# Decode step taken apart (new states made in the later convolutions and the inner out pairs) and 16 K tiles by Strassen in the heads

## The chip, the cores and the metric

One core of a Trainium2 chip runs the whole program. The metric is the device time of one execution in microseconds. The kernel before takes 2169.63 us, the median of three runs (2169.62 to 2169.96).

## The reference, cut to what matters

Two layers of a decoder trunk are run for a prompt of 512 tokens and for 8 decode samples of one token each; both share all weights, so the kernel carries 520 columns. Each layer has a wide input projection (8192 columns of K = 2048), a short convolution, a retention with 4 heads of 256, an output projection and a gate.

```python
def retention_chunk(S, q, k, v, log_gamma):
    ...
    scores = jnp.einsum('blhd,bmhd->bhlm', q, k) * decay[None]
    intra = jnp.einsum('bhlm,bmhe->blhe', scores, v)
    q_dec = jnp.exp(log_gamma[None, :] * (idx[:, None] + 1.0))
    inter = jnp.einsum('blhd,bhde->blhe', q, S) * q_dec[None, :, :, None]
    k_dec = jnp.exp(log_gamma[None, :] * (L - 1.0 - idx[:, None]))
    S_new = (jnp.exp(log_gamma * L)[None, :, None, None] * S
             + jnp.einsum('blhd,blhe->bhde', k * k_dec[None, :, :, None], v))
    return S_new, intra + inter

def trunk_layer(x, p_i, pos, conv_buf, ret_S, norm_g, w_in, conv_w, gn_g, w_out, w_pg, w_ple):
    h = rmsnorm(x, norm_g)
    z = h @ w_in
    ...
    y_conv = b_c * conv_y * jax.nn.silu(g_c)
    ...
    o, new_S = retention(q, k, v, ret_S.astype(jnp.float32), retention_log_gamma())
    ...
    x = x + jnp.concatenate([y_conv, y_ret], axis=-1) @ w_out
    x = x + jax.nn.sigmoid(x @ w_pg) * (p_i @ w_ple)
```

For a decode sample L is 1. Its new state is S' = gamma S + k v, and its output is o = q S'. There are 64 such states (2 layers x 4 heads x 8 samples), each 256 x 256 floats, 256 KB.

## The kernel before, in words

**Matmuls.** The operands stay in SBUF, transposed: 16 K tiles of 128 rows by 520 columns (512 tokens and 8 samples, in a LEFT and a RIGHT half of 260). A product in full precision is three matmuls: high part of the weights by high and by low part of the operand, and low part by high part (`mm3`, L247 to L249). A weight is loaded by SP into the ring `raw` (32 tiles), and split by ACT (`hi`, L229) and DVE (`lo`, L230) into the ring `split` (60 tiles). One call of `pair` makes two blocks of 128 output rows from two rows of weights. Its number `s` in the lists HEADS, CONVS, OUT_ROWS and GATES says how many of the 16 K tiles go through one level of Strassen's scheme: 7 products of s/2 tiles, and 4 sums of weights, which DVE adds in `raw` (L319) before they are split. The other 16 - s tiles go through four plain products. With s = 0 (`plain`) there is no scheme.

**Stages of a layer.** First the heads: 16 pairs (four per head: q, k, v, gate), with DVE and ACT work for rope, and the retention of the prompt in nine small steps per head, which `aside` takes from the list `later` in the middle and at the end of each pair. Then the convolutions: 8 steps j, each with two pairs. Then the out pairs (m = 0, 2, ..., 14), of which the first and the last have s = 0, then the gate pairs. Between stages the operands of the next one are built from tiles that POOL loads (`Operands.fill`, `build`: yc and ys for the out pairs), as slots come free. 75 slots of 128 x 520 hold operands, tiles and states.

**The decode step.** After a head's v is there, `todo` gets its 8 states. `sample` is called once or twice in a pair through the heads and the convolutions: it works on the state that was loaded at the call before, and loads the next one. A state needs two slots: the state (L770), and k and q of the sample, broadcast to all partitions (L771). ACT multiplies the state by gamma (L776), DVE adds k v in two halves (L780), POOL stores the new state (L781), and DVE multiplies it by q and sums (L784) into `osum`. `sample_norm`, in the last convolution, normalizes `osum` for the out pairs.

**What sets the order.** Each engine runs its instructions in one order, fixed when the program is built: a scheduler places them by their place in the code, by priorities (`WPRIO` puts weight splits ahead) and by its own estimate of when inputs are ready. `keep` pins an instruction behind what was traced before it on its engine. `middle` and `later` are lists of calls that a pair takes up at fixed points in it. SP's queue loads weights alone, but for the start and the end; all other loads and stores are issued by POOL, in one queue.

Of the kernel before, what the change touches and what calls it, by code (L numbers as in the profile page):

```python
# [7 lines left out]
F32 = mybir.dt.float32  # L8
# [5 lines left out]
P = 128  # L14
# [38 lines left out]
HEADS = [[0, 0, 0, 8] + [14] * 12, [0] + [14] * 15]  # L53
CONVS = [[14] * 2 + [16] * 13 + [14]] * 2
# [10 lines left out]
SPLIT = 60  # L65

# [125 lines left out]
def trunk_kernel(  # L192
# [368 lines left out]
    vec = const.tile([P, 160], F32, name="vec")  # L561
# [18 lines left out]
    def gam(h):  # L580
        return vec[:, 128 + h : 129 + h]

# [7 lines left out]
    osum = const.tile([P, 2, H, NS], F32, name="osum")  # L590
    gs = const.tile([P, 2 * H, NS], F32, name="gs")
# [83 lines left out]
    for a, b in ((0, 1), (1, 4), (4, 8), (8, 12), (12, 16)):  # L675
        raws = []
        if b == 1:
            raw = raw_ring.get(4)
            DMA.dma_start(raw.rearrange("p (m n) -> p m n", n=P), wi[0, 0:4, :, :P].rearrange("m p n -> p m n"))
            S.dma_start(vec, vecs)  # L680
# [35 lines left out]
    for l in range(DEPTH):  # L716
# [51 lines left out]
        def sample_load(h, b):  # L768
            st, kb = get(), get()
            SIDE.dma_start(st[:, :512], sret[l, h, b])  # L770
            SIDE.dma_start(kb[:, :512], kq[l, h, b].rearrange("c d -> (c d)").partition_broadcast(P))  # L771
            return h, b, st, kb

        def sample_step(h, b, st, kb):

            keep(S.activation(st[:, :512], st[:, :512], AF.Identity, scale=gam(h)))  # L776
            k = kb[:, 256:512]
            for e in range(2):
                c = slice(256 * e, 256 * e + 256)
                keep(V.scalar_tensor_tensor(st[:, c], k, vs[:, h, e, b : b + 1], st[:, c], MUL, ADD))  # L780
            SIDE.dma_start(o_rets[l, h, b], st[:, :512])  # L781
            for e in range(2):
                c = slice(256 * e, 256 * e + 256)
                V.tensor_tensor_reduce(k, st[:, c], kb[:, :256], 1.0, 0.0, MUL, ADD, osum[:, e, h, b : b + 1])  # L784
            put(st, kb)

        loaded = []
# [7 lines left out]

        todo = []
# [20 lines left out]
        def retain(h):  # L817
# [21 lines left out]
            aside_copy(h, 2, kf)  # L839
            qkt = small.tile([P, 4, 32], F32, tag="qkt", name="qkt")  # L840
# [6 lines left out]
            for e, z in enumerate(head(mt + 4)):  # L847
                t = z.slot if z.ps is None else copied(z.ps).slot
                V.scalar_tensor_tensor(vs[:, h, e, :], t[:, SEQ:T], 1.0 / 16, rb[:, SEQ:T], MUL, MUL)
# [227 lines left out]
        for j in range(CJ):  # L1077
            mt = 32 + 4 * j
            O.ready = min(j // 2, 3)
            middle.append(sample)  # L1080
            zc, zx = pair(X, wi[l], mt, mt // 2 - skipped, O)
            u = get()
# [18 lines left out]
            if j == CJ - 1:  # L1101
# [3 lines left out]
                sample_norm(nc, small, pr, osum, onesd, half_neg, gs, lambda k: gn_g(l, k))  # L1105
            zg, zb = pair(X, wi[l], mt + 2, mt // 2 + 1 - skipped, O)
            gt = silu(zg)
# [371 lines left out]
```

## Time and profile before

| | |
|---|---|
| median of three runs | 2169.63 us |
| span of the profiled execution, first to last instruction | 2167.3 us |
| PE busy | 2147.8 us |
| DVE busy | 1896.1 us |
| ACT busy | 1264.5 us |
| POOL busy | 430.6 us |
| read from HBM, written to it | 318.96 MB, 65.15 MB |

The profiled execution is given by its span; the 2.3 us between it and the median lie around it. By the lines that mark the stages, the heads of the first layer run to about 460 us, its convolutions to 710, its out pairs to 870 and its gates to 1110; the second layer's to about 1540, 1785, 1945 and 2130 us. Busy time of a matmul counts its whole way through the array, so that overlapping ones fill an engine's row; the counts (x) of a stretch tell how many were started. The granted clock is 1.00 of full speed in the stretches that are read below.

### The profile page before, as it was taken

What the parts mean: (1) busy time and instruction counts of PE and PEld (TensorE: products, weight loads), DVE (VectorE), ACT (ScalarE), POOL (GpSimd) and SP (SyncE); (2) the same over time, 40 slices, a digit from 0 to 9 for tenths busy, and PEclk for the clock granted to TensorE, in tenths of its full rate; (3) what the DMA queues carried; (4) which work ended last, traced back from release to release, by engine and by line L of the source; (5) the groups of instructions that cost most, each with busy time, mean ns of one, the idle gap of its engine ahead of it and who ended that gap; (6) DMA issues with size and microseconds to landing.
All of it is one profiled execution on the core that took longest, in us unless ns stands there. A gap on an engine that the chain in (4) does not pass through costs nothing. (4 is left out here: it accounts for less than half of the span.)

```text
span 2167.3 us, 48178 instructions
## 1 busy us (share of the span) xinstructions
PE 2147.8 (99%) x17861; PEld 2142.1 (99%) x17861; DVE 1896.1 (87%) x3849; ACT 1264.5 (58%) x2647; POOL 430.6 (20%) x746
## 2 busy tenths in 40 slices
PE   9999999999999999999999999999999999999998
PEld 9999999999999999999999999999999999999998
DVE  8889988998999987987997988989999998879884
ACT  8656655565555655655765655565645555456565
POOL 2313222211001211200212222231111022011011
PEclk9999999999999999999999999999999999999999
DMA  8555565545543745645645566664464355566455
GB/s 288 171 175 197 181 217 184 178 157 175 158 129 118 238 156 187 215 154 160 215 144 175 172 213 191 189 209 170 151 182 149 120 158 202 176 207 200 128 164 198
DMA packets 182861, 387.31 MB, mean 179 GB/s; under 512 B 25888, under 2 KB 56352, under 8 KB 182624
## 3 DMA queue, kind: packets, MB, share of 16 engines
q1 hardware_dynamic: 128704, 212.98, 31.6%
q0 software_dynamic: 53056, 169.84, 23.8%
q8 instruction: 140, 2.29, 0.4%
q10 hardware_dynamic: 864, 1.39, 0.2%
q14 instruction: 97, 0.79, 0.1%
HBM read 318.96 MB, written 65.15 MB: 177 GB/s over the span
## 5 line engine op out<-in xcount | busy, mean ns | idle before, releaser
L247 PE MATMUL ps_g<-slot,split 128*128 128x260 f32 x5465 | 1531.6, 284 | 7.2 <-ACT slot L307 2.9
L248 PE MATMUL ps_g<-slot,split 128*128 128x260 f32 x5465 | 1534.3, 282 | 0.3 <-DVE slot L555 0.3
L249 PE MATMUL ps_g<-slot,split 128*128 128x260 f32 x5461 | 1519.9, 283 | 0.5 <-DVE split L230 0.5
L229 ACT ACTIVATE split<-raw 128x512 fp32r<-128x512 f32 (+2 forms) x1347 | 777.3, 596 | 583.1 <-DVE raw L319 213.2
L247 PEld LDWEIGHTS ps_g<-slot,split 128*128 128x128 f32 x5465 | 1024.0, 188 | 10.1 <-ACT slot L307 3.7
L248 PEld LDWEIGHTS ps_g<-slot,split 128*128 128x128 f32 x5465 | 1028.5, 188 | 0.5 <-DVE slot L555 0.5
L249 PEld LDWEIGHTS ps_g<-slot,split 128*128 128x128 f32 x5461 | 1019.8, 188 | 1.0 <-DVE split L230 1.0
L230 DVE TENSOR_TENSOR split<-raw,split 128x512 fp32r<-128x512 f32 (+2 forms) x1346 | 849.2, 652 | 172.5 <-PE ps_g L248 85.4
L319 DVE TENSOR_TENSOR raw<-raw 128x512 f32<-128x512 f32 (+1 forms) x660 | 428.9, 660 | 32.5 <-DMA raw<-wi 23.7
L307 ACT ACTIVATE slot<-ps_g 128x260 f32<-128x260 f32 x336 | 127.4, 381 | 140.6 <-PE ps_g L249 122.7
L551 ACT ACTIVATE slot<-slot 128x520 fp32r<-128x520 f32 (+1 forms) x212 | 109.2, 562 | 46.6 <-DVE slot L414 11.1
L552 DVE TENSOR_TENSOR slot<-slot,slot 128x520 fp32r<-128x520 f32 (+1 forms) x212 | 124.4, 620 | 4.1 <-ACT slot L551 3.9
L781 POOL DMA_DIRECT2D o_rets<-slot x64 | 35.3, 552 | 351.6 <-DVE slot L780 131.7
L307 DVE TENSOR_TENSOR slot<-ps_g,slot 128x260 f32<-128x260 f32 x168 | 70.9, 424 | 6.0 <-PE ps_g L249 3.7
L869 POOL DMA_DIRECT2D slot<-hs x64 | 46.2, 724 | 118.7 <-DVE split L230 42.7
L814 POOL DMA_DIRECT2D hs<-slot x64 | 35.6, 556 | 139.3 <-DVE slot L755 61.3
L780 DVE SCALAR_TENSOR_TENSOR slot<-slot,vs,slot 128x256 f32<-128x256 f32 x128 | 56.1, 481 | 4.5 <-ACT slot L776 4.3
L746 DVE TENSOR_TENSOR slot<-slot,slot 128x520 f32<-128x520 f32 x80 | 55.8, 698 | 4.7 <-DMA o_rets<-slot 3.7
L770 POOL DMA_DIRECT2D slot<-sret x64 | 35.5, 554 | 114.6 <-ACT split L229 37.3
L1058 POOL DMA_DIRECT2D slot<-x1s x76 | 40.8, 538 | 87.6 <-PE ps_g L249 27.2
L1209 POOL DMA_DIRECT2D x2s<-slot x30 | 16.4, 545 | 201.6 <-DVE slot L1204 200.6
L771 POOL DMA_DIRECT2D slot<-kq x64 | 34.9, 547 | 106.0 <-DVE slot L876 22.2
(217 smaller groups left out, 1733.8 us busy)
## 6 DMA issues: line engine op xcount, KB each, us to landing
raw<-wi SPq DMA_DIRECT2D x377, 256.0 KB, 3.9
raw<-wo SPq DMA_DIRECT2D x128, 256.0 KB, 5.4
raw<-wg SPq DMA_DIRECT2D x122, 256.0 KB, 4.1
raw<-wi SPq DMA_DIRECT2D x136, 192.0 KB, 4.0
slot<-x1s POOLq DMA_DIRECT2D x76, 260.0 KB, 5.1
slot<-sret POOLq DMA_DIRECT2D x64, 256.0 KB, 4.0
hs<-slot POOLq DMA_DIRECT2D x64, 256.0 KB, 4.0
slot<-hs POOLq DMA_DIRECT2D x64, 256.0 KB, 5.2
```

Source lines behind the costliest of these rows:

```text
L229: S.activation(hi, raw, AF.Copy)
L230: V.tensor_tensor(lo, raw, F(hi), SUB)
L247: PE.matmul(out, wh, xh, start=start, stop=False, skip_group_check=more)
L248: PE.matmul(out, wh, xl, start=False, stop=False, skip_group_check=more)
L249: PE.matmul(out, wl, xh, start=False, stop=stop, skip_group_check=more)
L307: fn(*args)
L319: V.tensor_tensor(out[:, n], x[:, n], y[:, n], op)
L551: keep(S.activation(hi, src[:, n], AF.Copy))
L552: V.tensor_tensor(lo, src[:, n], F(hi), SUB)
L746: V.tensor_tensor(out[:, n], v, table[:, n], MUL)
L780: keep(V.scalar_tensor_tensor(st[:, c], k, vs[:, h, e, b : b + 1], st[:, c], MUL, ADD))
L869: SIDE.dma_start(t[:, :512].rearrange("p (m n) -> p m n", m=2), src)
```

## The change

The decode step is taken apart. With gamma folded into v (`vs` holds v / 16 / gamma), the new state is gamma (S + k v'), and the output is gamma q S + (gamma q k) v'.

- **Output.** `sample` loads the state alone, and the q of two samples at once (one slot for two states). DVE multiplies by q with the factor gamma and sums, twice per state; nothing is written to the state but the product. The part of k v' is added for all samples at once in `sample_norm`: two products of ones by `qk` on PE, and four small DVE operations.
- **New state.** `update` makes it later: in the convolutions from j = 3 twice in a pair, in the out pairs m = 2 to 12 three times. A call loads the broadcast k of one state (L798, `key_load`), multiplies the k that the call before had loaded by v' on ACT, half by half (L804), and issues a DMA that adds the old state from HBM to it in SBUF (L805, `accum_op=ADD`). Two calls after that ACT multiplies by gamma (L809) and POOL stores the state (L810).
- **Strassen.** 14 becomes 16 in 12 head pairs of the first layer and 15 of the second, and in the first two convolution pairs of both.

```diff
+GAMMA = [1.0 - 2.0 ** (-5 - h) for h in range(H)]
-HEADS = [[0, 0, 0, 8] + [14] * 12, [0] + [14] * 15]
-CONVS = [[14] * 2 + [16] * 13 + [14]] * 2
+HEADS = [[0, 0, 0, 8] + [16] * 12, [0] + [16] * 15]
+CONVS = [[16] * 15 + [14]] * 2
...
+UPDATES = 3
...
         def sample_load(h, b):
-            st, kb = get(), get()
+            st = get()
             SIDE.dma_start(st[:, :512], sret[l, h, b])
-            SIDE.dma_start(kb[:, :512], kq[l, h, b].rearrange("c d -> (c d)").partition_broadcast(P))
-            return h, b, st, kb
-
-        def sample_step(h, b, st, kb):
-
-            keep(S.activation(st[:, :512], st[:, :512], AF.Identity, scale=gam(h)))
-            k = kb[:, 256:512]
+            if b % 2 == 0:
+                queries.append(get())
+                src = kq[l, h, b : b + 2, :2].rearrange("b c d -> b (c d)").partition_broadcast(P)
+                SIDE.dma_start(queries[-1][:, :512].rearrange("p (b c) -> p b c", b=2), src)
+            return h, b, st, queries[-1]
+
+        def sample_step(h, b, st, q):
+
             for e in range(2):
                 c = slice(256 * e, 256 * e + 256)
-                keep(V.scalar_tensor_tensor(st[:, c], k, vs[:, h, e, b : b + 1], st[:, c], MUL, ADD))
-            SIDE.dma_start(o_rets[l, h, b], st[:, :512])
-            for e in range(2):
-                c = slice(256 * e, 256 * e + 256)
-                V.tensor_tensor_reduce(k, st[:, c], kb[:, :256], 1.0, 0.0, MUL, ADD, osum[:, e, h, b : b + 1])
-            put(st, kb)
-
-        loaded = []
+                n = slice(256 * (b % 2), 256 * (b % 2) + 256)
+                keep(V.tensor_tensor_reduce(st[:, c], st[:, c], q[:, n], GAMMA[h], 0.0, MUL, ADD, osum[:, e, h, b : b + 1]))
+            put(st)
+            if b % 2:
+                put(q)
...
+        def key_load(h, b):
+            st = get()
+            SIDE.dma_start(st[:, 256:512], kq[l, h, b, 2:].rearrange("c d -> (c d)").partition_broadcast(P))
+            return h, b, st
+
+        def state_add(h, b, st):
+            for e in range(2):
+                c = slice(256 * e, 256 * e + 256)
+                keep(S.activation(st[:, c], st[:, 256:512], AF.Copy, scale=vs[:, h, e, b : b + 1]))
+            SIDE.dma_start(st[:, :512], sret[l, h, b], accum_op=ADD)
+            return h, b, st
+
+        def state_out(h, b, st):
+            keep(S.activation(st[:, :512], st[:, :512], AF.Copy, scale=GAMMA[h]))
+            SIDE.dma_start(o_rets[l, h, b], st[:, :512])
+            put(st)
+
+        keyed, added = [], []
+
+        def update():
+
+            if len(added) > 1 or added and not (keyed or states):
+                state_out(*added.pop(0))
+            if keyed:
+                added.append(state_add(*keyed.pop(0)))
+            if states:
+                keyed.append(key_load(*states.pop(0)))
...
+            V.scalar_tensor_tensor(qk[:, :, h], qks[:, :2, :NS], GAMMA[h], qks[:, 2:, :NS], MUL, MUL)
...
+            if j >= UPDATES:
+                middle.append(update)
             zc, zx = pair(X, wi[l], mt, mt // 2 - skipped, O)
+            if j >= UPDATES:
+                update()
...
+            busy = 0 < m < KT - 2
+            if busy:
+                middle.append(update)
+                later.append(update)
             zs = pair(O, wo[l], m, m // 2, Gt)
+            if busy:
+                update()
...
+    for d in range(2):
+        PE.matmul(ps[:, :n], ones, qk[:, d].rearrange("p h b -> p (h b)"), start=d == 0, stop=d == 1)
+    own = small.tile([P, 2, H, NS], F32, tag="sq", name="own", bufs=1)
+    for e in range(2):
+        V.tensor_tensor(own[:, e], vs[:, :, e], ps[:, :n].rearrange("p (h b) -> p h b", b=NS), MUL)
+        V.tensor_tensor(osum[:, e], osum[:, e], own[:, e], ADD)
```

**How it moves instructions.** On DVE, in a head pair of the first layer, before: weight splits of 3 and 4 tiles (128x384, 128x512) and of the two plain tiles (128x256), and between them a decode step with its add (L780) and its two products (L784, each followed by a read of its sum).

```order
L230 TENSOR_TENSOR split_73<-raw_72,split_73 128x512
L230 TENSOR_TENSOR split_73<-raw_72,split_73 128x384
L984 SCALAR_TENSOR_TENSOR shift_2030<-mv_2027,rstp_2029 128x2
L230 TENSOR_TENSOR split_73<-raw_72,split_73 128x512
L780 SCALAR_TENSOR_TENSOR slot65_174_1910<-slot30_175_1911,vs_81,slot65_174_1910 128x256 x2
L230 TENSOR_TENSOR split_73<-raw_72,split_73 128x256 x2
L784 ISA slot30_175_1911,osum_82<-slot65_174_1910,slot30_175_1911 128x256
```

On DVE at such a place of the change (its lines are shifted: L232 is L230, L321 is L319, L782 is L784):

```order
L232 TENSOR_TENSOR split_73<-raw_72,split_73 128x512
L948 SCALAR_TENSOR_TENSOR slot65_196_2319<-ps_kt_2313,vec_74,slot60_195_2318 128x256
L782 ISA slot10_181_2015,osum_82<-slot10_181_2015,slot56_182_2017 128x256
L782 ISA osum_82 128x1
L782 ISA slot10_181_2015,osum_82<-slot10_181_2015,slot56_182_2017 128x256
L782 ISA osum_82 128x1
L232 TENSOR_TENSOR split_73<-raw_72,split_73 128x512 x5
L321 TENSOR_TENSOR raw_72<-raw_72 128x512
```

The adds and the pieces of 2 and 3 tiles are gone; all pieces have 4 tiles.

On POOL, where the convolutions of the first layer go over into the out pairs, the row of the change holds loads of yc and ys (operands of the out pairs), loads of xT (their residuals), and of the update the store o_rets, the accumulating load from sret and the key load from kq:

```order
L810 DMA o_rets<-slot65_447_8721 128x512
L1093 DMA slot44_516_9362<-ys_93 128x512
L1171 DMA slot46_542_9695<-xT 128x520
L1088 DMA slot53_526_9542<-yc_89 128x520
L805 DMA slot68_452_8965<-sret 128x512
L1171 DMA slot52_525_9427<-xT 128x520
L1093 DMA slot0_532_9557<-ys_93 128x512
L1093 DMA slot70_531_9554<-ys_93 128x512
L1171 DMA slot45_541_9694<-xT 128x520
L810 DMA o_rets<-slot14_451_8900 128x512
L805 DMA slot38_493_9254<-sret 128x512
L798 DMA slot11_522_9417<-kq_92 128x256
```

Before, POOL's row holds there the loads of yc, ys and xT alone:

```order
L1058 DMA slot21_477_9343<-yc_88 128x520
L1058 DMA slot29_478_9345<-yc_88 128x520
L1118 DMA o_conv<-ncv_79 128x144
L1063 DMA slot59_490_9374<-ys_92 128x512
L1063 DMA slot66_489_9371<-ys_92 128x512
L1063 DMA slot20_508_9501<-ys_92 128x512
```

On ACT, in an out pair of the change (L231 are the weight splits, L309 copies out of PSUM, L553 operand splits), one state, slot52_554, from its two copies with v' to its last copy:

```order
L804 ACTIVATE slot52_554_9818<-slot52_554_9818,vs_81 128x256
L231 ACTIVATE split_73<-raw_72 128x512 x2
L309 ACTIVATE slot47_543_9702<-ps_g_9700 128x260
L804 ACTIVATE slot52_554_9818<-slot52_554_9818,vs_81 128x256
L553 ACTIVATE slot67_558_9977<-slot0_556_9971 128x520
L553 ACTIVATE slot44_560_9981<-slot58_557_9972 128x520
L231 ACTIVATE split_73<-raw_72 128x512 x3
L309 ACTIVATE ps_g_10009<-ps_g_10007 128x260
L231 ACTIVATE split_73<-raw_72 128x512
L809 ACTIVATE slot52_554_9818<-slot52_554_9818 128x512
```

Four weight splits stand between the second L804, on which the accumulating DMA waits, and L809, which waits for that DMA. Before, none of the L804 and L809 rows are there, and nothing in their place.

More of the change, by code (lines that the diff above doesn't have):

```diff
@@ L558, in split @@
         return op
-    vec = const.tile([P, 160], F32, name="vec")
+    vec = const.tile([P, P], F32, name="vec")
     def norm_g(l, k):
@@ L578, in kd @@
         return vec[:, c : c + 1]
-    def gam(h):
-        return vec[:, 128 + h : 129 + h]
     ident = const.tile([P, P], F32, name="ident")
@@ L590, in trunk_kernel @@
     osum = const.tile([P, 2, H, NS], F32, name="osum")
+    qk = const.tile([P, 2, H, NS], F32, name="qk")
     gs = const.tile([P, 2 * H, NS], F32, name="gs")
@@ L679, in trunk_kernel @@
             DMA.dma_start(raw.rearrange("p (m n) -> p m n", n=P), wi[0, 0:4, :, :P].rearrange("m p n -> p m n"))
-            S.dma_start(vec, vecs)
+            S.dma_start(vec, vecs[:, :P])
             x = get()
@@ L768, in sample_load @@
         def sample_load(h, b):
[L769 removed]
+            st = get()
             SIDE.dma_start(st[:, :512], sret[l, h, b])
[L771 to L777 removed]
+            if b % 2 == 0:
[4 more added lines that the diff above has]
+        def sample_step(h, b, st, q):
             for e in range(2):
                 c = slice(256 * e, 256 * e + 256)
[L780 to L787 removed]
+                n = slice(256 * (b % 2), 256 * (b % 2) + 256)
[3 more added lines that the diff above has]
+                put(q)
+        loaded, queries = [], []
         def sample():
@@ L794, in sample @@
                 loaded.append(sample_load(*todo.pop(0)))
+        def key_load(h, b):
[20 more added lines that the diff above has]
+                keyed.append(key_load(*states.pop(0)))
+        states = [(h, b) for h in range(H) for b in range(NS)]
         todo = []
@@ L1104, in trunk_kernel @@
                 O.ready = 7
-                sample_norm(nc, small, pr, osum, onesd, half_neg, gs, lambda k: gn_g(l, k))
+                sample_norm(nc, small, pr, osum, qk, vs, ones, onesd, half_neg, gs, lambda k: gn_g(l, k))
+            if j >= UPDATES:
+                middle.append(update)
             zg, zb = pair(X, wi[l], mt + 2, mt // 2 + 1 - skipped, O)
+            if j >= UPDATES:
+                update()
             gt = silu(zg)
@@ L1135, in trunk_kernel @@
             middle.append(lambda: O.fill(MORE_OUT, 0))
+            busy = 0 < m < KT - 2
+            if busy:
+                middle.append(update)
+                later.append(update)
             zs = pair(O, wo[l], m, m // 2, Gt)
+            if busy:
+                update()
             for i, (x, z) in enumerate(zip(xs, zs)):
@@ L1359, in trunk_kernel, with sample_norm @@
             block_out(1)
+        assert not (todo or loaded or states or keyed or added)
         if l < DEPTH - 1:
             X.ready = KT // 2
-def sample_norm(nc, small, pr, osum, onesd, half_neg, gs, gn):
+def sample_norm(nc, small, pr, osum, qk, vs, ones, onesd, half_neg, gs, gn):
     V, G, PE = nc.vector, nc.gpsimd, nc.tensor
@@ L1368, in sample_norm @@
     flat = osum.rearrange("p e h b -> p e (h b)")
+    ps = pr.tile([P, 512], F32, tag="r", name="ps_qk")
+    for d in range(2):
[4 more added lines that the diff above has]
+        V.tensor_tensor(osum[:, e], osum[:, e], own[:, e], ADD)
     ps = pr.tile([P, 512], F32, tag="r", name="ps_sm")
```

2 lines of the change are left out of this document (1 added, 1 removed).

## The prediction

> **What bounds the kernel now.** I read the engine shares first, then the busy times by stretch, then the groups by form, and last the DMA answer.
>
> ```profile
> PE 2147.8 (99%) x17861; PEld 2142.1 (99%) x17861; DVE 1896.1 (87%) x3849; ACT 1264.5 (58%) x2647; POOL 430.6 (20%) x746
> ```
>
> PE is busy 99%, but matmuls overlap, so this alone could hide a PE that is fed late. Starts per stretch decide. In the rows below the columns are stretch, length, then PE, weight load, DVE, ACT and POOL busy with their counts, granted clock, DMA share, GB/s.
>
> ```profile
> 640.00:660.00 20.00, 20.00 (x170) 20.00 (x169) 18.64 (x38) 10.98 (x21) 1.08 (x2) 1.00 0.46 133
> 1060.00:1080.00 20.00, 20.00 (x169) 20.00 (x168) 19.80 (x46) 18.98 (x38) 5.87 (x11) 1.00 0.78 258
> 1080.00:1100.00 20.00, 20.00 (x169) 20.00 (x168) 19.85 (x44) 18.51 (x37) 5.88 (x11) 1.00 0.72 230
> ```
>
> PE starts 169 or 170 matmuls in 20 us whether DVE is busy 18.6 or 19.85 of them, ACT 11 or 19, DMA 0.46 or 0.78. So the pace is PE's own: 20 us / 169 = 118.3 ns a matmul, and a matmul less is 118.3 ns less as long as feeding holds. Where it doesn't hold is seen in few places; the worst are the changes from the convolutions to the out pairs, one in each layer (700 and 1780 us).
>
> ```profile
> 700.00:730.00 30.00, 26.68 (x218) 26.07 (x218) 30.00 (x65) 24.88 (x68) 10.58 (x20) 1.00 0.81 272
> 1780.00:1800.00 20.00, 18.15 (x149) 17.72 (x149) 19.66 (x44) 13.67 (x38) 6.77 (x13) 1.00 0.94 333
> ...
> 720.00:726.00 6.00, 5.30 (x45) 5.10 (x43) 6.00 (x13) 6.00 (x18) 2.31 (x5) 1.00 1.03 376
> 726.00:732.00 6.00, 4.58 (x35) 4.37 (x36) 6.00 (x14) 4.14 (x12) 1.07 (x2) 1.00 0.98 357
> ```
>
> PE loses 3.3 us in the first and 1.85 us in the second. There the DMA engines are full (1.03, 0.98), DVE has no gap and ACT is full for 6 us at a time.
>
> **16 tiles by Strassen, on PE.** A pair with s = 14 issues 7 products of 7 tiles and 2 tiles in four plain products, 3 matmuls each: 147 + 24 = 171. With s = 16 it is 7 x 8 x 3 = 168. The lists change 27 pairs in the heads and 2 per layer in the convolutions: 31 x 3 = 93 matmuls, and 93 x 118.3 ns = **-11.0 us**, all on PE's path.
>
> **The same on DVE.** It pays for it:
>
> ```profile
> L230 DVE TENSOR_TENSOR split<-raw,split 128x512 fp32r<-128x512 f32 x1031 | 695.0, 690 | 147.8 <-PE ps_g L248 81.2 <-ACT split L229 51.8 <-issue 6.1
> L319 DVE TENSOR_TENSOR raw<-raw 128x512 f32<-128x512 f32 x520 | 354.1, 688 | 17.6 <-DMA raw<-wi 12.1 <-DMA raw<-wo 2.9
> L230 DVE TENSOR_TENSOR split<-raw,split 128x384 fp32r<-128x384 f32 x249 | 137.1, 555 | 16.2 <-ACT split L229 9.9 <-PE ps_g L248 3.4 <-ACT slot L551 1.9
> L319 DVE TENSOR_TENSOR raw<-raw 128x384 f32<-128x384 f32 x140 | 77.4, 554 | 14.9 <-DMA raw<-wi 11.6 <-DMA raw<-wg 2.8
> L780 DVE SCALAR_TENSOR_TENSOR slot<-slot,vs,slot 128x256 f32<-128x256 f32 x128 | 56.1, 481 | 4.5 <-ACT slot L776 4.3
> ...
> L230 DVE TENSOR_TENSOR split<-raw,split 128x256 fp32r<-128x256 f32 x66 | 27.3, 423 | 8.5 <-ACT split L229 7.6 <-PE ps_g L248 0.8
> ```
>
> Splits per pair: 7 x (690 + 555) + 2 x 423 = 9.56 us before, 14 x 690 = 9.66 us after. Sums of weights: 4 x (688 + 554) = 4.97 us before, 8 x 688 = 5.50 us after. That is 0.64 us more in each of 31 pairs, 19.8 us. The decode step gives back its two L780 a state: 128 x 481 ns = 61.6 us by means (56.1 busy, since they overlap). Where they run (DVE busy with L780 alone):
>
> ```profile
> 66.00:410.00 344.00, 17.57 (x40) 1.00 0.59 190
> ...
> 1110.00:1480.00 370.00, 17.56 (x40) 1.00 0.59 184
> ```
>
> So DVE does some 36 us less in all (56.1 - 19.8), and in the heads 27 x 0.64 = 17 us more against 35 less.
>
> ```profile
> 66.00:460.00 394.00, 394.00 (x3289) 393.53 (x3288) 357.23 (x774) 234.63 (x515) 102.58 (x178) 1.00 0.58 185
> 460.00:710.00 250.00, 247.85 (x2069) 247.48 (x2068) 228.30 (x454) 138.68 (x282) 36.67 (x54) 1.00 0.49 148
> 710.00:870.00 160.00, 157.88 (x1314) 157.45 (x1313) 134.96 (x248) 85.92 (x183) 26.82 (x50) 1.00 0.60 195
> ```
>
> DVE has 37 us idle in the first head stage already (394 - 357), and the convolutions ran 13 of their 16 pairs with s = 16 beside 228 of 250 us of DVE. I cost the DVE part at nothing; if that cover were gone it would be 17 us, and the 35 us stand against it. No more slots are taken: the operands are shared with the convolutions, whose rows of 16 had all eight sums built before.
>
> **The state update on ACT and POOL.** Per state ACT loses one L776 early and gains two half copies with a scale and one full copy later. The trace doesn't have these; the nearest rows:
>
> ```profile
> L776 ACT ACTIVATE slot<-slot,vec 128x512 f32<-128x512 f32 x64 | 45.7, 714 | 0.0
> L917 ACT ACTIVATE slot<-ps_kt,vec 128x256 fp32r<-128x256 f32 x32 | 15.0, 468 | 9.2 <-DMA hs<-slot 3.2 <-DVE slot L918 2.5 <-PE ps_kt L913 2.2
> L874 ACT ACTIVATE slot<-slot 128x512 fp32r<-128x512 f32 x48 | 28.7, 624 | 10.1 <-DMA yc<-slot 4.6 <-DVE slot L904 2.4 <-DVE osum L784 2.1
> L770 POOL DMA_DIRECT2D slot<-sret x64 | 35.5, 554 | 114.6 <-ACT split L229 37.3 <-PE ps_s L249 13.8 <-ACT slot L307 9.7
> ```
>
> 2 x 468 + 624 = 1.56 us an update (1.65 with L776's for the last copy). An out pair has up to three calls: 4.7 us beside 85.9 / 160 x 20 = 10.7 us of ACT in 20. ACT holds that. POOL issues 96 more DMAs (64 accumulating, 64 of keys, 32 of queries for 64 of L771): 96 x 554 ns = 53 us of an engine that is idle 80%. Hidden. What is new is who waits: the accumulating DMA waits on POOL for ACT's two copies, the store of o_rets for its last one, and behind them in POOL's queue stand key loads, the residual loads of the out pairs and their x1s stores, for which the next pair's slots wait.
>
> **The DMA engines.**
>
> ```profile
> q0 software_dynamic: 53056, 169.84, 23.8%
> ...
> slot<-sret POOLq DMA_DIRECT2D x64, 256.0 KB, 4.0
> ```
>
> Queue 0 moves 169.84 MB in 23.8% of 16 engines' span: 0.238 x 2167.3 / 169.84 = 3.04 us a MB, or 0.80 us for 256 KB. An accumulating DMA isn't in this trace. It reads HBM, and SBUF too: 0.80 us if the second read is free, 1.6 us if it costs a load and a store. I take 0.80, its nearest row, and keep both.
> The Trainium skill (Collectives: The Full Stack, "The bandwidth ceiling: the fold count and why AG ≠ RS ≠ AR") says that an adding transfer is slow not by its add but by its two source reads; by that the upper value holds, and no row here shows it. By that rule the sum below would be about 2 x 2.4 us higher, 2169 us.
>
> An update moves 256 + 256 + 128 KB: 2.0 us. In the convolutions (DMA 0.49) and in the out pairs (0.60) that is 3 x 2.0 = 6 us in 20, up to 0.9 of the engines, about what 1060 us has without loss. I cost it at nothing there.
>
> At the **change of stage** it isn't free. By the order, between the store of o_conv and that of the last yc, POOL issues three o_rets stores, three accumulating DMAs and four key loads: 6 x 0.80 + 4 x 0.40 = 6.4 us (8.8 by the upper value). The 30 us from 700 have 0.19 x 30 = 5.7 us of DMA idle and 5.1 of ACT, and three updates need 4.7 of ACT. So it just fits on paper, in a stretch where PE waits anyway and yc and ys loads stand behind o_rets in one POOL queue. Loss: at best less than now (the order has fewer operand splits ahead of the last convolution's copies on ACT), at worst all 8.8 us. I take 2.5 us in each layer, near the overflow (0.7 to 3.1), **+5.0 us**.
>
> **The small sums.** ps_qk adds 8 small matmuls:
>
> ```profile
> L1371 PE MATMUL ps_sm<-osum,onesd x8: 191/275/276, 664.7 to 1734.8; 128*128 128x32 f32 x8
> ```
>
> They overlap, and have an eighth of the columns of a matmul of 118.3 ns; I take 90 ns each, **+0.7 us** (0 to 8 x 0.275 = 2.2). The order has ps_sm 800 matmuls behind ps_qk, so the four small DVE rows between are waited for by nobody.
>
> **Sum**, on the profiled execution: 2167.3 - 11.0 + 0.7 + 5.0 = 2162.0. Its span is 2.3 us below the median of the runs, 2169.6; I carry that along: **2164 us**.
>
> **The rivals.**
> *The change of stage costs nothing:* for it speak 1060 to 1100 us, as loaded and without loss. 2167.3 - 11.0 + 0.7 + 2.3 = 2159.3.
> *It costs twice as much:* loads queue behind o_rets stores that wait for ACT, which waits for an accumulating DMA. 5.5 us a layer: 2170. For it: DMA at 1.03 there already.
> *The added wait becomes the bound (slower).* On ACT the last copy of a state waits for its accumulating DMA, and behind it on ACT stand the weight splits that PE needs. By the order 17 states have seven splits or fewer between the two, often five; 14 splits go to a pair of 19.9 us, so five are 7.1 us.
>
> ```profile
> L770 POOL DMA_DIRECT2D slot<-sret x64: 537/544/585, 50.5 to 1670.9; - x64
> ...
> DMA to landing us min/median/max: 2.8/4.0/7.3
> ```
>
> A plain load lands in 4.0 us, 7.3 at most, and at that nothing waits. But an out pair has 20 - 15.4 = 4.6 us of ACT idle and 1.4 such states: from a landing of 7.1 + 4.6 / 1.4 = 10.4 us on PE falls behind, by 1.4 x 12 pairs = 17 us for each us more. The point from which the kernel is slower than before is 10.7 us; at 12 us it costs 27 us: 2191. Against it: that is 2.6 times a plain load's median.
> *DVE sets the pace, not PE* (the 93 matmuls then count for nothing, and the change works by DVE): the heads would shorten by up to 35 - 17 = 18 us, 2155. The steady 169 starts speak against it.
>
> **How the numbers follow.** Forecast 0.38, no cost at the change 0.22, twice the cost 0.24, the slower rival 0.13, DVE 0.03. A measurement of this kernel can tell about 0.2% (4.3 us) from no change: faster is below 2165.3, slower above 2174.0. Faster gets 0.22, 0.03 and 0.30 of the forecast's 0.38: 0.55. Same gets the other 0.08 and most of the doubled cost: 0.31. Slower gets 0.13 and a rest: 0.14. The range runs from the rival without cost, less 3 us if PE loses less there than the 3.3 and 1.85 us of now, 2156, to the doubled cost with the upper bound of the DMAs (2167.3 - 11.0 + 0.7 + 2 x 8.8 + 2.3 = 2176.9), 2177.
>
> **What would show it.** PE rows fall by 85 (93 - 8), with 118.3 ns still between starts, and pairs in the heads at 19.9 us. DVE busy falls by about 36 us, ACT rises. In the 30 us around 700 and 1780 PE's loss grows from 3.3 and 1.85 by some 2.5 each. The accumulating DMAs land in 4 to 8 us, and ACT waits for few of them. I am wrong if the head stages lose PE time, if landings pass 10 us, or if the out pairs show PE idle where they had none.

## The result and the profile after

The changed kernel takes 2202.76 us (median of five runs, 2196.15 to 2209.13), the kernel before 2169.63 in the same job (five runs, 2166.32 to 2169.96). The ratio is 1.016 with a 95% interval of 1.0141 to 1.0179: slower by 33 us, and 39 us above the forecast. The sign was wrong, and the time lies outside the range. Two executions on record, one of experiment 2 (5762.05 us) and one of experiment 5 (7419.09 us), ran in a slower state of the chip and are left out of the times below.

The page of the changed kernel, first its engine shares, then its two large DMA queues (packets, MB, share of 16 engines; q1 carries SP's transfers, the weights, and q0 POOL's, states, keys and activations):

```profile
PE 2149.2 (98%) x17776; PEld 2136.5 (97%) x17776; DVE 1876.2 (85%) x3675; ACT 1299.8 (59%) x2682; POOL 512.4 (23%) x842
...
q1 hardware_dynamic: 119776, 212.98, 30.1%
q0 software_dynamic: 62784, 186.63, 28.0%
```

PE has the 85 rows less that were expected (17861 - 17776) and DVE 20 us less (36 were forecast), so no engine has grown into a bound by its sum. Queue 0 has grown from 23.8% to 28.0%, and in a longer span.

To find the place I took the starts of three landmark rows of DVE: the second shifted product of the first and of the last convolution of a layer (L1093 before, L1127 after), and the last addition of its residual in the out pairs (L1139, L1183). They cut the profiled execution into stages, in us. These landmarks are rows of DVE, and PE's own stream moves a little against them, so the last two columns count the matmuls that PE starts in a stage, and PE's lost time: the length of the stage less 118.3 ns for each matmul started.

| stage | before | after | difference | matmuls, difference | lost time, difference |
|---|---|---|---|---|---|
| start to the first convolution (heads of layer 0) | 411.7 | 406.9 | -4.8 | -55 | +1.7 |
| convolutions, layer 0 | 303.4 | 306.3 | +2.9 | -12 | +4.2 |
| last convolution to the last out pair, layer 0 | 182.1 | 200.2 | +18.1 | +32 | +14.3 |
| gates of layer 0 and heads of layer 1 | 585.6 | 576.2 | -9.4 | -79 | -0.2 |
| convolutions, layer 1 | 300.2 | 307.1 | +6.9 | +8 | +6.0 |
| last convolution to the last out pair, layer 1 | 184.1 | 204.4 | +20.3 | +10 | +19.2 |
| the rest | 200.2 | 200.0 | -0.2 | +11 | -1.5 |

The heads gained 14 us, but only because PE starts 134 matmuls fewer between their landmarks (15.9 us); the lists of 16 explain 81 of them (27 pairs x 3, 9.6 us). Time is lost where the updates are: 10.2 us in the convolutions and 33.5 in the two stages of out pairs. The same columns as in the prediction, for stretches of the change:

```profile
1060.00:1110.00 50.00, 50.00 (x420) 50.00 (x419) 44.36 (x96) 42.70 (x85) 14.93 (x28) 1.00 0.81 263
...
570.00:700.00 130.00, 126.99 (x1044) 125.58 (x1042) 109.81 (x213) 78.05 (x166) 34.03 (x43) 1.00 0.62 175
...
690.00:760.00 70.00, 63.21 (x493) 61.38 (x491) 55.83 (x123) 43.77 (x107) 27.98 (x39) 0.95 0.71 231
730.00:740.00 10.00, 8.03 (x42) 7.27 (x43) 10.00 (x24) 9.70 (x25) 1.98 (x3) 0.66 1.04 337
...
780.00:850.00 70.00, 64.36 (x521) 62.70 (x520) 53.16 (x92) 44.82 (x95) 25.72 (x42) 1.00 0.82 226
```

And the kernel before in four of these stretches:

```profile
570.00:700.00 130.00, 130.00 (x1088) 130.00 (x1087) 118.98 (x237) 69.53 (x138) 12.39 (x13) 1.00 0.43 130
...
690.00:760.00 70.00, 66.68 (x552) 66.05 (x551) 63.57 (x132) 42.21 (x104) 17.12 (x32) 1.00 0.67 215
730.00:740.00 10.00, 10.00 (x86) 10.00 (x85) 9.30 (x20) 3.97 (x10) 2.77 (x6) 1.00 0.65 193
...
780.00:850.00 70.00, 70.00 (x586) 70.00 (x585) 57.53 (x96) 34.38 (x65) 6.46 (x12) 1.00 0.49 160
```

From 690 to 760 us, around the change from convolutions to out pairs, PE starts 493 matmuls instead of 552. Part of that is the clock: behind PE's waits there its granted clock has a mean of 0.66 from 730 to 740 us (42 matmuls, 86 before), and 0.95 over the 70 us, which is 3.5 us of full clock. In the kernel before it is 1.00.

From 780 to 850 us PE starts 521 matmuls instead of 586. No engine is full there: DVE has 53 of 70 us, ACT 45. The DMA engines went from 0.49 to 0.82. But 0.81 costs nothing at 1060 us, so the share alone doesn't say it. The DMA answer, cut to a stretch of convolutions, shows more (issues, KB each, median us from issue to landing). Before, from 570 to 700 us:

```profile
raw<-wi SPq DMA_DIRECT2D x47, 256.0 KB, 3.5
```

After, in the same stretch:

```profile
raw<-wi SPq DMA_DIRECT2D x44, 256.0 KB, 6.5
slot<-sret POOLq DMA_DIRECT2D x15, 256.0 KB, 6.5
```

The weights land 3 us later. The sum of two weights on DVE, which is the first to touch a landed weight (L319 before, L321 after), shows it as idle time; for wi and wo together 26.6 us before, 55.6 after:

```profile
L319 DVE TENSOR_TENSOR raw<-raw 128x512 f32<-128x512 f32 (+1 forms) x660 | 428.9, 660 | 32.5 <-DMA raw<-wi 23.7 <-DMA raw<-wo 2.9 <-DMA raw<-wg 2.8
L321 DVE TENSOR_TENSOR raw<-raw 128x512 f32<-128x512 f32 (+1 forms) x660 | 441.7, 680 | 59.2 <-DMA raw<-wi 36.6 <-DMA raw<-wo 19.0 <-DMA raw<-wg 0.5
```

One such place, from the chain of waits of the change between 825 and 850 us (start, us, what):

```profile
831.25 0.69 DVE split L232
831.97 9.33 DMA raw<-wo
841.55 0.44 issue
842.00 0.43 DVE slot L309
842.47 0.39 PE ps_g L249
```

A load of weights took 9.33 us, and PE went on only behind it. That is one place; in the out pairs the median landing hardly moves (5.8 us before and 6.1 after, from 780 to 850 us). What waits for the adding transfer itself is small. All instructions of its line (L805), who waited for them, and their landing:

```profile
L805 POOL DMA_DIRECT2D slot<-sret x64: 849/882/1272, 537.8 to 1950.0; - x64
...
  ACT slot L809: 13.0, 7
...
DMA to landing us min/median/max: 4.0/6.7/11.2
```

So after the first look two theories stood: the adding transfers crowd the weights out (A), or the waits of ACT and POOL behind them pass on to PE (B, the prediction's slower rival). The letters in the expectations below are each run's own. And Strassen's part had to be priced by itself.

### The profile page after: what moved, and what is told of

The parts are those of the page before. It is cut to its first block, busy times and chain, and to the rows that moved or that the text cites. A ratio compares the mean times of both kernels' runs of the same rounds, so it can differ in the third digit from the quotient of the medians.

```text
span 2201.0 us, 47748 instructions
## 1 busy us (share of the span) xinstructions
PE 2149.2 (98%) x17776; PEld 2136.5 (97%) x17776; DVE 1876.2 (85%) x3675; ACT 1299.8 (59%) x2682; POOL 512.4 (23%) x842
## 4 chain that ended last, share of the span: by engine, by line
PE 75%; DMA 10%; DVE 5%; issue 5%; ACT 3%; POOL 1%; DVEq 0%; SPq 0%; POOLq 0%; ACTq 0%
PE ps_g L249 23%; PE ps_g L251 23%; PE ps_g L250 23%; DMA raw<-wi 5%; DMA raw<-wo 2%; DVE split L232 2%; DVE raw L321 2%; ACT split L231 1%; DMA slot<-yc 1%; ACT slot L804 1%; DMA slot<-sret 1%; ACT slot L809 1%; PE ps_p L249 1%; PE ps_p L250 1%; PE ps_p L251 1%
## 5 line engine op out<-in xcount | busy, mean ns | idle before, releaser
L231 ACT ACTIVATE split<-raw 128x512 fp32r<-128x512 f32 (+1 forms) x1285 | 779.5, 623 | 555.0 <-DVE raw L321 306.7
L249 PEld LDWEIGHTS ps_g<-slot,split 128*128 128x128 f32 x5434 | 1018.9, 188 | 47.8 <-DVE slot L309 14.6
L232 DVE TENSOR_TENSOR split<-raw,split 128x512 fp32r<-128x512 f32 x1284 | 851.7, 680 | 190.7 <-PE ps_g L250 97.6
L321 DVE TENSOR_TENSOR raw<-raw 128x512 f32<-128x512 f32 (+1 forms) x660 | 441.7, 680 | 59.2 <-DMA raw<-wi 36.6
L309 ACT ACTIVATE slot<-ps_g 128x260 f32<-128x260 f32 x336 | 128.2, 382 | 159.7 <-PE ps_g L251 140.3
L553 ACT ACTIVATE slot<-slot 128x520 fp32r<-128x520 f32 (+1 forms) x212 | 109.4, 562 | 40.4 <-DVE slot L416 10.9
L309 DVE TENSOR_TENSOR slot<-ps_g,slot 128x260 f32<-128x260 f32 x168 | 70.6, 421 | 5.1 <-PE ps_g L251 4.8
L770 POOL DMA_DIRECT2D slot<-sret x64 | 35.7, 559 | 160.3 <-ACT split L231 24.6
L805 POOL DMA_DIRECT2D slot<-sret x64 | 57.3, 895 | 67.6 <-ACT slot L804 36.8
L810 POOL DMA_DIRECT2D o_rets<-slot x64 | 36.8, 575 | 135.6 <-ACT slot L809 125.5
L798 POOL DMA_DIRECT2D slot<-kq x64 | 37.5, 587 | 132.4 <-DMA o_rets<-slot 46.6
L804 ACT ACTIVATE slot<-slot,vs 128x256 f32<-128x256 f32 x128 | 63.7, 498 | 1.1 <-DMA slot<-kq 1.1
L1088 POOL DMA_DIRECT2D slot<-x1s x76 | 41.1, 542 | 87.8 <-PE ps_g L251 33.5
```

What stands on the lines that cost most here:

```text
L231: S.activation(hi, raw, AF.Copy)
L232: V.tensor_tensor(lo, raw, F(hi), SUB)
L249: PE.matmul(out, wh, xh, start=start, stop=False, skip_group_check=more)
L309: fn(*args)
L321: V.tensor_tensor(out[:, n], x[:, n], y[:, n], op)
L553: keep(S.activation(hi, src[:, n], AF.Copy))
```

## The experiments

Each ratio is to the kernel before in the same job; the medians of before were 2168.92 (the first four), 2168.60 (the next three), 2168.46 (the next three) and 2167.44 us (the last).

**1. A plain load in place of the adding one.** The instructions stand in the same order on every engine.

```diff
-            SIDE.dma_start(st[:, :512], sret[l, h, b], accum_op=ADD)
+            SIDE.dma_start(st[:, :512], sret[l, h, b])
```

> The changed kernel with a plain load of the old state in place of the accumulating one; the order of every engine's instructions is the same, row for row. The new states lack the k v part. Theory A (the accumulating DMA itself: it lands later, 6.7 us by median against 3.9 for the plain sret loads of the decode step, and holds back the weight loads beside it, 6.4 against 4.1 us): the 44 us between the forecast and the change go for the most part, 2160 to 2172 us. Theory B (the added traffic of 256 KB and 128 KB loads at that place, whatever their kind): 2190 us or more. Theory C (added rows on ACT and waits in POOL's queue): 2190 us or more.

2178.52 us, ratio 1.0056 (1.0035 to 1.0078), between the theories. The adding alone is worth 24.2 us of the 33, but the rest is more than theory A expected: a plain second load isn't free either.

**2. No second load at all.** The line is left out.

```diff
-            SIDE.dma_start(st[:, :512], sret[l, h, b], accum_op=ADD)
```

> The changed kernel without the second load of the old state (the new states are k v alone); the scheduler places other instructions anew. Theory A: as with the plain load, within 5 us of it, 2158 to 2170 us. Theory B: only this one gets near 2160 us, the plain load doesn't. Theory C: 2185 us or more, since ACT's rows and the stores in POOL's queue remain.

2166.96 us, ratio 0.9994 (0.9984 to 1.0004). The plain load is 11.6 us of the change, the adding load 35.8. Theory C is out; of A and B neither holds as it stands, since both the load and its kind count. From 780 to 850 us this kernel starts 585 matmuls, as before, with the key loads, both kinds of copies on ACT and the o_rets stores in place:

```profile
780.00:850.00 70.00, 70.00 (x585) 69.93 (x584) 58.09 (x98) 45.93 (x95) 18.38 (x34) 1.00 0.67 217
```

But the rest of the change isn't free. This kernel, too, starts 85 matmuls fewer than the kernel before, 10.1 us, and its span is only 0.8 us shorter (2166.5 for 2167.3). So PE loses 9.3 us more than before without any second load, 3.3 and 7.0 us of it in the stages of out pairs (190.1 and 193.7 us). Whether keys, copies, stores or the order make that wasn't taken apart.

**3. Strassen's lists alone, in the kernel before.**

```diff
-HEADS = [[0, 0, 0, 8] + [14] * 12, [0] + [14] * 15]
-CONVS = [[14] * 2 + [16] * 13 + [14]] * 2
+HEADS = [[0, 0, 0, 8] + [16] * 12, [0] + [16] * 15]
+CONVS = [[16] * 15 + [14]] * 2
```

> The kernel before with the Strassen lists of the change alone. If PE sets the pace and DVE's gaps hold the 17 us that the heads' pairs add: 93 matmuls less, 2159 us. If DVE has no room in the heads without the decode step's relief: 2167 us or more.

2186.00 us, ratio 1.0077 (1.0057 to 1.0096): 17.1 us slower, where 11 us were to be gained. The loss lies in the heads: start to the first convolution 422.5 us (before 411.7), gates and heads of layer 1 592.7 (585.6). The first heads of this kernel:

```profile
66.00:400.00 334.00, 324.09 (x2666) 321.98 (x2665) 301.29 (x614) 189.29 (x388) 92.32 (x158) 0.99 0.56 184
```

And of the kernel before:

```profile
66.00:400.00 334.00, 334.00 (x2788) 333.53 (x2787) 301.68 (x659) 199.83 (x441) 93.16 (x162) 1.00 0.59 190
```

DVE is busy for the same 301 us of 334 and PE starts 122 matmuls fewer beside it. Its 33 us idle were no room for more work; what held them open wasn't taken apart. The granted clock is 0.99 here, 3 us of full clock in 334.

**4. The change with the old lists.** The same four lines the other way.

> The change with the Strassen lists of before, so the decode step alone. If the two parts add up, it is the 2203 us of the change plus 11: 2208 to 2218 us. If the longer pairs with 16 have a part in the loss: below 2203 us.

2206.28 us, ratio 1.018 (1.0159 to 1.02). That lies between the two cases that were expected. By the medians the lists of 16 bring the change 3.5 us, but the intervals of the two ratios overlap. Its two head stages take 408.5 and 581.0 us, so 7.8 of the 14 us that the heads gained come with the decode step, and 6.4 with the lists.

**5. Two plain loads in place of the adding one.**

```diff
-            SIDE.dma_start(st[:, :512], sret[l, h, b], accum_op=ADD)
+            SIDE.dma_start(st[:, :512], sret[l, h, b])
+            d = get()
+            SIDE.dma_start(d[:, :512], sret[l, h, b])
+            put(d)
```

> The change with each accumulating DMA replaced by two plain 256 KB loads of the old state, one into the slot of the new state and one into a spare slot that is given back at once (the new states then lack the part k v', as in the run with one plain load). Theory A: what the accumulating DMA costs is its time on the DMA engines, by its packets 128 x 178 ns = 22.8 us of one engine or 1.42 us of all 16, against 64 x 161 ns = 0.64 us for a plain load. Two plain loads are 1.29 us, so the kernel comes near the change: 2192 to 2204 us. Theory B: it is something of the adding itself (a longer hold of a queue, the later landing that ACT or POOL wait for). Then two plain loads cost about twice what one did, 11 us each by the two runs before: 2184 to 2190 us.

2191.49 us, ratio 1.0103 (1.0083 to 1.0122), half a microsecond below theory A's range and above B's. The queue row of this kernel:

```profile
q0 software_dynamic: 63808, 203.41, 28.0%
```

With the rows of the other kernels, share times span gives the engine time of queue 0:

| second transfer of a state | queue 0 | x span | more than none, a state | weights (wi) land, 570 to 700 us | DVE idle for wi and wo in its sums (128x512) | kernel |
|---|---|---|---|---|---|---|
| none (experiment 2) | 23.9% | 517.8 us | | 4.0 us | 9.6 us | 2167.0 us |
| one plain load (1) | 26.1% | 568.0 us | 0.78 us | 5.3 us | 30.7 us | 2178.5 us |
| two plain loads (5) | 28.0% | 614.2 us | 1.51 us | 6.2 us | 37.7 us | 2191.5 us |
| one adding load (the change) | 28.0% | 616.3 us | 1.54 us | 6.5 us | 47.8 us | 2202.8 us |

The times rise with every column. An adding load takes the engines as long as two plain ones; the trace's packet records say why: 128 packets of 2 KB at 178 ns (median), against 64 of 4 KB at 159 ns for a plain load. Two plain loads, with the same engine time, account for 24.5 of the 35.8 us (2191.5 - 2167.0). The last 11 us belong to the adding in some other way. POOL takes 882 ns to issue one, and 539 for a plain load, so two plain ones hold POOL longer still and that isn't it. What it is stays open.

The way from engine time to PE is shown less well than the price. In the convolutions the weights land later, step by step. In the out pairs, where most is lost, their landing doesn't order the kernels: from 780 to 850 us wo lands in 5.7, 6.1, 6.6 and 6.1 us (medians, in the order of the table), while PE starts 585, 562, 541 and 521 matmuls. And a part passes through the clock: the mean granted clock of an execution was 0.997 to 0.999 without a second load, 0.995 or 0.996 with plain ones and 0.992 to 0.997 with the adding one, and 0.003 of 2180 us is 6.5 us. No run separates the clock from the waits that go with it.

**6. The update in place, half of it on ScalarE** (the kernel before with the lists of 16):

```diff
-            keep(S.activation(st[:, :512], st[:, :512], AF.Identity, scale=gam(h)))
-            k = kb[:, 256:512]
+            k, kv = kb[:, 256:512], get()
             for e in range(2):
                 c = slice(256 * e, 256 * e + 256)
-                keep(V.scalar_tensor_tensor(st[:, c], k, vs[:, h, e, b : b + 1], st[:, c], MUL, ADD))
+                keep(S.activation(kv[:, c], k, AF.Copy, scale=vs[:, h, e, b : b + 1]))
+            keep(V.scalar_tensor_tensor(st[:, :512], st[:, :512], gam(h), kv[:, :512], MUL, ADD))
+            put(kv)
```

> The kernel before with the change's lists of 16, and with the update of a state in place by one VectorE instruction of 512 columns (old state times decay plus k v'), where ScalarE makes k v' in two halves; no second load and no accumulating DMA. VectorE has 2 x 481 ns less and about 0.70 us more, 0.26 us a state or 17 us in all, as much as the lists of 16 add in the heads; ScalarE has 0.28 us a state more. Theory A: the lists of 16 alone were slower because VectorE in the heads had no room for 17 us more. Then most of the loss of 17 us goes and some of the 93 matmuls shows: 2160 to 2172 us. Theory B: it was the feeding of weights (one pair of 16 holds all 32 tiles of the ring, and loads come later), which VectorE's time doesn't touch: 2182 to 2188 us.

2185.19 us, ratio 1.0079 (1.0062 to 1.0095), no better than the lists alone, as theory B had it. But the test was weaker than planned. In the groups by form the new instruction is

```profile
L780 DVE SCALAR_TENSOR_TENSOR slot<-slot,vec,slot 128x512 f32<-128x512 f32 x64 | 47.6, 744 | 1.4 <-ACT slot L779 1.3
```

against 56.1 us of the two that it replaces: DVE got 8.5 us back, not 17, where the lists ask for 24 (L230 and L319 together went from 1278.1 us before to 1301.8 in experiment 3). It tells little between the theories.

**7. The lists of 16 without VectorE's two additions** (the loop of two `scalar_tensor_tensor` above left out).

> The kernel before with the change's lists of 16, and without VectorE's two additions of k v' to each state (128 instructions, 56 us): the new states hold the old ones times the decay, and the output of the decode step lacks its own k v' part. All transfers and their places stay. Theory A, VectorE's room in the heads decides whether 16 pays: 2155 to 2163 us, the 93 matmuls in full. Theory B, the ring of weights and its loads decide: 2180 to 2187 us, as with the lists alone.

2162.41 us, ratio 0.9971 (0.9959 to 0.9982): 23.6 us faster than experiment 3, with the same weights, ring and transfers, and the first of these kernels that is faster than the kernel before. With 56 us less of DVE, the lists pay. (The read-outs and the store behind those additions start earlier too; that was not taken apart.) They pay 6 us, not the whole 11: the heads of layer 0 now take 409.8 us for 411.7.

**8. The additions on GpSimd** (the lists of 16, k v' on ScalarE):

```diff
-                keep(V.scalar_tensor_tensor(st[:, c], k, vs[:, h, e, b : b + 1], st[:, c], MUL, ADD))
+                keep(S.activation(kv[:, c], k, AF.Copy, scale=vs[:, h, e, b : b + 1]))
+            keep(nc.gpsimd.tensor_tensor(st[:, :512], st[:, :512], kv[:, :512], ADD))
+            put(kv)
```

> The kernel before with the change's lists of 16; ScalarE scales the old state by the decay and makes k v' in two halves, and GpSimd adds the two (one instruction of 512 columns a state) in place of VectorE's two additions. Nothing is loaded twice. Theory A, VectorE's room in the heads decides: VectorE is relieved of the same 56 us as in the run without the additions, which gave 2162.4 us, and ScalarE, idle by 40% there, pays 1 us a state: 2158 to 2168 us, a kernel with the reference's outputs that beats both. Theory B: GpSimd's add is slow or gets in the way of VectorE, whose operations read two operands from SBUF too, or holds up the transfers that GpSimd issues: 2180 us or more, with VectorE's own instructions longer than 688 ns.

2190.12 us, ratio 1.0097 (1.0068 to 1.0126). Theory B held. The line of GpSimd's addition, its duration and who waited:

```profile
L781 POOL TENSOR_TENSOR slot<-slot,slot x64: 1264/1308/5487, 107.8 to 1733.1; 128x512 f32<-128x512 f32 x64
...
  POOL o_rets L783: 13.6, 30
  DVE slot L786: 7.3, 6
```

And the weight splits of this kernel, in the groups by form:

```profile
L230 DVE TENSOR_TENSOR split<-raw,split 128x512 fp32r<-128x512 f32 x1248 | 865.6, 707 | 164.6 <-PE ps_g L248 107.0 <-ACT split L229 37.9 <-issue 8.7
```

GpSimd needs 1308 ns for its addition where VectorE's instruction of experiment 6 took 744 for the same columns, VectorE waits for it (7.3 us), and VectorE's own splits went to 707 ns a piece (690 before): 1248 x 17 ns = 21 us of the 56 are given back by longer instructions. The other 35 us don't show in the time; POOL's own additions stand before its stores and loads, and what they cost there wasn't taken apart.

The Trainium skill (SBUF — State Buffer, "Who interferes with whom") says that a VectorE instruction with two inputs in SBUF contends with a GpSimd instruction that reads SBUF. The trace agrees: the splits and the addition are of these kinds, and the splits got longer.

**9. The decay one call later.**

```diff
-            if len(added) > 1 or added and not (keyed or states):
+            if len(added) > 2 or added and not (keyed or states):
```

> The change with the decay one more call late (three calls behind the accumulating DMA instead of two), at one slot more. Theory A: what is lost is lost to late weights, and few instructions wait for the accumulating DMA itself (ScalarE 13 us in 7 places): 2197 to 2206 us, no change. Theory B, the slower rival of the prediction: ScalarE waits for the landing and holds the weight splits behind it. Then most of the 13 us and what they cause goes: 2180 to 2192 us.

2202.71 us, ratio 1.0159 (1.0144 to 1.0174), no change. The line of the decay in this kernel:

```profile
L809 ACT ACTIVATE slot<-slot x64: 611/622/635, 557.6 to 1966.0; 128x512 f32<-128x512 f32 x64
...
its engine sat idle before it (us, times) until:
who waited for it (us, times):
  POOL o_rets L810: 106.7, 28
```

Nothing stands under "idle before it": ACT waits for no adding load any more, and the kernel takes as long. The slower rival's mechanism, ACT held by landings, wasn't at work. POOL still waits 106.7 us for ACT before its stores, so this run says little of POOL's queue.

**10. Updates in the convolutions only.**

```diff
-        states = [(h, b) for h in range(H) for b in range(NS)]
+        states = [(h, b) for h in range(H) for b in range(NS)][:17]
```

> The change with the updates of 17 states a layer only, so that they all lie in the convolutions and at most one call is left for the first out pair; the new states of the other 15 aren't made or stored. Theory A, the place decides: out pairs have little room between weights that are loaded and split in time, and three updates a pair are too many there; convolutions lose 3 to 6 us a layer. The out stages come back to 180 to 185 us: 2162 to 2172 us in all. Theory B, each accumulating update costs the same 0.55 us wherever it is (35 us over 64): 30 of them less are 16 us, 2184 to 2190 us.

2177.77 us, ratio 1.0044 (1.0027 to 1.006), between the theories. The 30 updates that went were worth 25.0 us, 0.83 each, but with their keys, copies and stores; all 64 second loads cost 0.56 each on the average. The out stage of layer 1 is back at 184.4 us, and that of layer 0 at 190.0; the convolutions stay at 309 each, about 10 us above the 299 of the kernel without a second load. For the second loads alone, the stages of the change against those of experiment 2 give 15.7 us for the 34 in the convolutions and 20.8 for the 30 in the out stages, 0.46 and 0.69 each. So the out pairs are the dearer place, but the convolutions pay as well.

Beginning the updates in the first convolution (`UPDATES = 0`), so that most of them lie in the convolutions, was meant as a run of its own: 2170 to 2182 us was expected if the place decides, 2196 to 2206 if each transfer costs the same anywhere. That kernel could not be built, since no slot was free for the operands of the retention of the prompt, so nothing was measured.

**11. A plain load and VectorE for decay and addition.**

```diff
-            SIDE.dma_start(st[:, :512], sret[l, h, b], accum_op=ADD)
+            old = get()
+            SIDE.dma_start(old[:, :512], sret[l, h, b])
...
-            keep(S.activation(st[:, :512], st[:, :512], AF.Copy, scale=GAMMA[h]))
+            keep(V.scalar_tensor_tensor(st[:, :512], old[:, :512], GAMMA[h], st[:, :512], MUL, ADD))
```

(and v' no longer divided by gamma).

> The change with a plain load of the old state into a slot of its own in place of the accumulating DMA, and with decay and addition in one VectorE instruction of 512 columns (744 ns, as measured in the run with the update in place) in place of ScalarE's copy with the decay (622 ns). The outputs are the reference's. Theory A, the transfer engines' time decides in the late stages: one plain load gave 2178.5 us; VectorE gains 64 x 0.74 = 48 us there, ScalarE loses 40 us, which about cancel: 2174 to 2186 us. Theory B, VectorE (0.83 to 0.87 busy in the convolutions, 0.76 to 0.83 in the out pairs) has no room there either: 2190 us or more, nothing gained over the accumulating DMA.

2188.00 us, ratio 1.0082 (1.0056 to 1.0108), between the two: 15 us faster than the change, 10 slower than the plain load of experiment 1. DVE's wait for weights in its sums is small here:

```profile
L321 DVE TENSOR_TENSOR raw<-raw 128x512 f32<-128x512 f32 x644 | 435.1, 688 | 15.2 <-DMA raw<-wo 9.5 <-DMA raw<-wi 2.7 <-DMA raw<-wg 0.2
```

So DVE waits little for weights, and the time now goes elsewhere in the out stages, which take 200.2 and 195.1 us. One stretch, from the waits of PE between 740 and 860 us:

```profile
PE ps_g L249 <- ACT slot L309: 3.4, 1, 3.4
PE ps_g L249 <- ACT slot L553: 3.1, 1, 3.1
```

PE waits for ACT, for a copy out of PSUM and for an operand. What ends those is not settled. No version here that does the whole computation beats the kernel before.

## Why the prediction was wrong, point by point

**Strassen on PE, -11.0 us: the count was right, the time held in part.** 85 rows went. By experiment 4 the lists brought 6.4 us in the heads, where 9.6 were forecast, and 3.5 us in all, if anything.

**"I cost the DVE part at nothing; if that cover were gone it would be 17 us": the cover was real and so was the price, too small.** Without the relief the lists came out 28 us from their -11 (experiment 3), with 24 us more of DVE. I took DVE's 37 us idle in the heads for room, which it wasn't, with DVE at 0.90 busy. That DVE's time alone decides isn't shown: 8.5 us less of it (experiment 6) and 35 us less (experiment 8) brought nothing, and in experiment 7 (56 us less) the stores and read-outs no longer stood behind the additions either. In the change the relief came along (L780 gone), so this step didn't sink the forecast; but as an independent term it was mis-sized, and DVE as a pace beside PE's was worth more than a chance of 0.03.

**The accumulating DMA, "I take 0.80, its nearest row": this size was wrong.** The queue rows give 1.54 us, the upper bound of 1.6. The rule of two source reads that the prediction named from the Trainium skill (Collectives: The Full Stack, "The bandwidth ceiling: the fold count and why AG ≠ RS ≠ AR") asked for that value, and the trace agrees with its price: an adding load takes as long as two plain ones. By it alone the sum would have been 2169, still 34 us short.

**"In the convolutions (DMA 0.49) and in the out pairs (0.60) ... I cost it at nothing there": this is the step that failed.** I argued from 1060 us that a share of 0.9 costs nothing. But the rows that I showed have 0.78 and 0.72 there, so nothing as full as 0.9 had been seen without loss. PE's lost time grew by 10.2 us in the convolutions and by 33.5 in the stages of out pairs; some 13 of these lie at the change of stage, which had a term, and 31 where I had put nothing. This is the last sign of being wrong that the prediction lists, PE idle in the out pairs.

How much comes in beside it doesn't settle it either. The change itself loads from 1060 to 1100 us, with a DMA share of 0.81 and no loss,

```profile
raw<-wi SPq DMA_DIRECT2D x14, 256.0 KB, 4.2
raw<-wg SPq DMA_DIRECT2D x4, 256.0 KB, 5.0
```

18 tiles of weights in 40 us, and the kernel before from 780 to 850 us

```profile
raw<-wo SPq DMA_DIRECT2D x26, 256.0 KB, 5.8
```

26 in 70 us, 15 in 40. What makes the same share harmless in one stretch and dear in the other stays open. The price is known: by the table of experiment 5 0.78 us of engine time a state cost 11.6 us, and 1.51 cost 24.5. A forecast with 1.54 us a state and that rate (24.5 / (64 x 1.51) = 0.25 us for each us) would have had +25 for the second loads where I had +5, and 11 us of the adding would still be missing.

**The change of stage, +5.0 us: the right place, too small.** In 70 us around the last convolution PE starts 59 matmuls fewer in layer 0 (493 for 552) and 51 fewer in layer 1 (516 from 1770 to 1840 us, for 567 from 1760 to 1830 before): 13.0 us, more than the doubled cost of the rival (11), and 3.5 of it are the lower clock. The chain of waits there runs over the loads of yc and POOL's issues, as the prediction feared (window 715 to 750 us; start, us, what):

```profile
709.96 7.37 DMA slot<-yc
...
717.86 6.18 DMA slot<-yc
...
732.48 0.87 POOL slot L805
```

Without the second loads (experiment 2) the same places have 13 and 25 matmuls fewer, 4.5 us, so 5.0 was near the price of the rest.

**ACT and POOL, "ACT holds that": right for ACT.** The two half copies take 498 ns each (468 taken), the last one 622, and ACT waited 13.0 us in all for adding loads. The waits of POOL behind ACT (125.5 us for L809) went to 106.7 in experiment 9 at the same time; whether the rest of them matters isn't shown. POOL's 96 issues took 82 us more (512.4 - 430.6), not 53.

**The slower rival had the sign, not the mechanism.** It asked for landings of over 10.4 us; they are 6.7 at the median, and PE falls behind all the same, though ACT waits for none of them in experiment 9.

**The range.** I listed the upper bound of the accumulating DMA's time and carried it only through the change of stage. Carried through all 64 updates it would have been 25 us more, at a rate that no row of before could give.

## What to carry to other kernels

A transfer that is moved off a busy engine is not free because the DMA engines have a share left: look at what else loads in that stretch, how long it takes to land, and who waits for it first. A load that adds took the DMA engines as long as two loads and cost more than two; a second plain load of the same 256 KB cost 12 us in 64 times here, so the update in place with what is loaded already was the cheaper one. And when an engine at 90% sits beside a full PE, take it as a second bound until an experiment relieves it: the same lists were 17 us slower with DVE's additions and 6 us faster without. Choose the stretch for a suspected stall wide enough, and read its clock: the stall at the change of stage ran on past 730 us.

## What the runs showed of the hardware

An adding load of 256 KB on POOL's queue moves in 128 packets of 2 KB, a plain one in 64 of 4 KB; POOL issues it in 882 ns for 539, and it lands in 6.7 us at the median for 5.4 in the same places (experiment 1). GpSimd's addition of two 128x512 tiles takes 1308 ns at the median, and while 64 such additions are in the kernel VectorE's weight splits of 128x512 take 707 ns on the average for 690, and its sums of weights 698 for 689 (experiments 8 and 3). PE's granted clock fell to a mean of 0.66 from 730 to 740 us of the change, behind waits of PE, and to 0.99 over the first heads of experiment 3.
